# Weights as the moving side: 128-token blocks stationary, 512 weight columns streamed, results with tokens on partitions

## The chip, the cores and the metric

The kernel runs on one core of a Trainium2 chip. The metric is device time in microseconds (us), the median of several executions. One execution was also recorded by the hardware profiler. Its engines are called PE (matrix products), DVE (elementwise, vector), ACT (elementwise with function tables), POOL (here only start values and DMAs that add) and SP (which only issues DMAs). Each engine works through its own instructions in order; an instruction that waits for a semaphore holds up all that follow it on that engine.

## The reference

One layer of a gated encoder trunk, for 512 tokens of width 2048, all in float32:

```
hn    = rmsnorm(x, norm_g)
proj  = hn @ w_in          # 12 heads x (q, k, v, g), 4 forget logits, 3 x 2048 merge gates
gates = sigmoid(proj[merge] + b_gate)
y[n]  = attention_n(q, k, v) * silu(g)       # n = A (forgetting), B (relative bias), C (stick-breaking)
out   = x + (sum_n gates[n] * (y[n] @ w_up[n])) @ w_out
```

A and B normalise every head's q and k over its 128 channels. Each head has 128 channels and there are 4 heads in each of the three branches. The products with `w_in` (12,288 columns and 4 logits), `w_up` (3 times 512 to 2048) and `w_out` (2048 to 2048) are nearly all of the work.

## The kernel before, in words

**Precision.** Every operand of a large product is split into a high and a low part of a shorter float type (`split`, L242: ACT copies the high part, L245; DVE subtracts it, L249). A product is then three: high x high, high x low, low x high.

**Which side moves.** On PE one operand is loaded into the array (stationary, 128 x 128) and the other streams through it. Here a 128 x 128 block of the weight is stationary, `wh` or `wl`, and the activations stream: results have 128 weight columns on partitions and tokens along the row, so q, k, the gate and the merge gates come out channel by channel.

**Strassen tasks.** `PairTask` (L602) takes two column blocks of 128 (q and k of a head, v and g of a head, two neighbouring merge gates, two output blocks) and forms them for the 512 tokens in seven products instead of eight: tokens in two halves of 256, the inner dimension in two halves of 8 x 128, the two column blocks as the third pair. The token sides of the products are the tiles x1, x2, t23, t4 (for the input) and m1, m2, m23, m4 (for the output), made once by DVE and ACT (`combos`, L505; `merged_a`, L1382, and `merged_b`, L1390). The weight sides are sums of 128-column blocks: two of the five loads of a task are followed by a POOL DMA that adds a second block, and DVE makes two more sums (L640, L646).

One product is one **unit**: 8 wide matmuls (L264, `wh` stationary, 512 columns streamed: 256 of the high and 256 of the low part of the token side) and 8 narrow ones (`wl` stationary, 256 columns of the high part). A unit's weights are one raw tile of 128 x 1024, split one or two units ahead of PE (`LA` = 2). There are 52 pair tasks, so 364 units. The products are put together on DVE and ACT (`after_of`, L692: copies, adds, and folds of two halves of 256).

**The stages.** (1) `first_quad`: q, k, v, g of head C0 straight from the unscaled x, four column blocks at a time, no Strassen; `norm_x` meanwhile finds each token's 1/rms, PE spreads it over all partitions (L479), and DVE multiplies x by it (`split_n`, L500) and splits x again. (2) Four merge gate blocks, no Strassen. (3) 44 pair tasks with the attention of 12 heads slipped in between. In A and B `normed` (L885) squares q and k, sums over channels with a matrix of ones on PE (L898, L899), and takes 16 times a chain of seven ACT and five DVE operations of 128 x 512. v is transposed on PE (L1058). (4) `up_units`: y times `w_up`, gated by the sigmoid of the merge gates, added over the branches: 16 blocks. (5) 8 output pair tasks; the first one in the order 1, 5, 2, 3, 6, 7, 4 (`late`), because its sixth token side m23 needs the last block of stage 4.

**What sets the order.** Nothing is scheduled by the compiler. At build time a planner (`Flow`) simulates PE, ACT and DVE with a fixed cost per operation (`mm_us`, `act_us`, `dve_us`) and a model of the DMA queue (`landing`, `add_up`), always takes the task that could start first, and the instructions are written in that order. Tile pools are counted (`Slots`): t2 are rows of 128 x 512, x the split token sides, raw the loaded weights (6 buffers), wh and wl their parts (3 buffers each), acc and att four PSUM banks each.

Of the kernel before, what the change touches and what calls it, by code (L numbers as in the profile page):

```python
# [8 lines left out]
F32 = mybir.dt.float32  # L9
# [6 lines left out]
P = 128  # L16
# [9 lines left out]
UK = 8  # L26
NQ = 4
# [135 lines left out]
def hybrid_kernel(  # L163
# [5 lines left out]
    w_first: bass.AP,  # L169
    w_col: bass.AP,  # L170
    rel: bass.AP,
# [25 lines left out]
    accs = [Slots(2), Slots(1), Slots(1)]  # L197
# [7 lines left out]
    def acc(i=0):  # L205

        return pa.tile([P, S], F32, tag=f"acc{i}", name=nm("acc"), bufs=1 if i else 2)
# [16 lines left out]
    class Parts:  # L224
# [10 lines left out]
        def both(self, i):  # L235

            return self.t[:, i, :, :], self.t[:, i, 0, :], self.ev[i]
# [57 lines left out]
    bg = small_in[:, KT + 5:KT + 5 + NB * DT]  # L295
    wf = small_in[:, KT + 5 + NB * DT:].rearrange("p (k h) -> p k h", h=NH)
# [9 lines left out]
    ones_r = cp.tile([P, P], F32R, name="ones_r")  # L306
    nc.vector.tensor_copy(ones_r, onef)
# [20 lines left out]
    t2s.free.pop()  # L328
# [8 lines left out]
    cur = [0]  # L337

    def at(u, g):
        side.setdefault(u, []).append(g)  # L340

    class Unit:


        def __init__(self, mms, after=None, shape=(UK, P), srcs=()):
# [3 lines left out]
        def source_there(self):  # L349
            return self.there  # L350

        def source(self):
            return self.raw
# [3 lines left out]

    def raw_tile(shape=(UK, P)):
        return wp.tile([P] + list(shape), F32, tag="raw", name=nm("raw"), bufs=NR)

    def load_unit(u):
        if isinstance(u, Pair):
            if u is u.task.units[0]:
                yield from u.task.load()
            return
        for s in u.srcs:
            yield raws, 1
            t = raw_tile(u.shape)
            to = t
            if len(s.shape) > len(t.shape):  # L370
                to = t.rearrange("p (c k) m -> p c k m", c=s.shape[1])
            u.raw = t
            u.there.t = fetch(to, s, flow.ready, 4 * u.shape[0] * P * P // 1024).t

    def prep(u):
        n = u.shape[0] * P
        u.hi = wp.tile([P] + u.shape, F32R, tag="wh", name=nm("wh"), bufs=LA + 1)
        u.lo = wp.tile([P] + u.shape, F32R, tag="wl", name=nm("wl"), bufs=LA + 1)
        yield u.source_there()
        yield from split(u.hi, u.lo, u.source(), n, u.ready, hi_ev=u.ready_hi)  # L380
        u.split_done()
# [7 lines left out]
    norm_ev = [Event() for _ in range(KT)]  # L389
    used_q = [Event() for _ in range(KT)]  # L390
    scaled, f_used = [Event() for _ in range(KT)], [Event() for _ in range(KT)]
    used_g = [Event() for _ in range(UK)]
    x1 = [Parts("x1", [norm_ev[k], Event()]) for k in range(UK)]
    x2 = [Parts("x2", [norm_ev[k + UK]] * 2) for k in range(UK)]
# [12 lines left out]
    xnat = [xp.tile([P, 2, S], F32, tag="x", name=nm("xn")) for _ in range(UK)]  # L407
    n_in = [Event() for _ in range(NQ * QB)]
# [28 lines left out]
    def rsqrt(y, ps, n, tmp, size, done=None):  # L437

        t, w, v = tmp
        yield ACT, act_us(size)  # L440
        nc.scalar.activation(t, ps, AF.Ln, bias=epsc, scale=1.0 / n)
        yield ACT, act_us(size)
        nc.scalar.activation(v, ps, AF.Identity, bias=nhepsc, scale=-0.5 / n)
        if done is not None:
            done()
# [9 lines left out]
    rstd, rstd_ev = [], Event()  # L455
    n_split = [0]

    def norm_x():
# [7 lines left out]
        small_n = cp.tile([P, 5, QB], F32, name="small_n")  # L466
        y, m, tmp = small_n[:, 0, :], small_n[:, 1, :], [small_n[:, i, :] for i in range(2, 5)]
        yield DVE, 0.2
        nc.vector.tensor_reduce(m, ssq, axis=AX.X, op=ALU.add)
        yield from rsqrt(y, m, D, tmp, 4)  # L470
        yield t2s, 1
        dg = t2("dg")
        for b in range(QB):
            yield ACT, 0.3
            nc.scalar.activation(dg[:, blk(b)], identf, AF.Copy, scale=y[:, b:b + 1])
        yield atts, 1
        ps = att()
        yield PE, 0.9
        nc.tensor.matmul(ps, onef, dg, start=True, stop=True)  # L479
        give(t2s, 2)  # L480
        yield t2s, 1
        yield ACT, act_us(S)
        rstd.append(t2("rstd"))
        nc.scalar.activation(rstd[0], ps, AF.Copy)
        give(atts)
        set_(rstd_ev)

    def rstd_used():
        n_split[0] += 1
        if n_split[0] == KT + 5:  # L490
            give(t2s)

    def split_n(kt):

        due = (52.0 + 1.0 * kt + (8 if kt >= UK else 0),)
        yield raw_ev[kt]
        yield rstd_ev
        yield f_used[kt]
        yield (DVE, dve_us(S), *due)
        nc.vector.tensor_mul(xraw[kt], xraw[kt], rstd[0])  # L500
        yield used_q[kt]
        yield from split(xs[kt].hi, xs[kt].lo, two(xraw[kt]), S, norm_ev[kt], due)
        rstd_used()

    def combos(k):  # L505

        due = (96.0 + k,)
        late = (106.0 + k,)
        yield norm_ev[k]
        yield norm_ev[k + UK]  # L510
# [10 lines left out]
        yield used_g[k]  # L521
        h, lo, ev = x1[k].half(1)
        yield from split(h, lo, a[:, LH], HS, ev, due)
# [6 lines left out]
        give(t2s)  # L530
        if k % 2 == 0:
            t4[k // 2] = Parts("t4")
# [4 lines left out]
        give(t2s)  # L537
# [3 lines left out]
    def strassen_ops(x1, x2, t23, t4):  # L541

        def part(ts, i):
            return lambda k: ts[k] and ts[k].both(i)

        return {1: part(x1, 0), 2: part(x2, 0), 3: part(x2, 1), 5: part(x1, 1), 6: part(t23, 0), 7: part(t23, 1),
                4: lambda k: t4[k // 2] and t4[k // 2].both(k % 2)}


    def halves(c):  # L550
        return [w_col[c, 0], w_col[c, 1]]

    def col_task(srcs, evac, bank=0, used=None):

        st = {}

        def mms(i):
            def go(u):
                if i == 0:
                    yield accs[bank], 1  # L560
                    st["ps"] = acc(bank)
                ps = two(st["ps"])
                for j in range(UK):
                    kt = i * UK + j
                    yield norm_ev[kt]
                    yield PE, mm_us(S, 2)
                    mm(ps, u.hi[:, j, :], xs[kt].hi, kt == 0)
                    mm(ps, u.hi[:, j, :], xs[kt].lo)
                yield u.ready
                for j in range(UK):  # L570
                    kt = i * UK + j
                    yield PE, mm_us(S)
                    mm(ps, u.lo[:, j, :], xs[kt].hi, stop=kt == KT - 1)
                    if used is not None and i == 0:
                        set_(used[j])
            return go

        def after():
            yield from evac(st["ps"])
            give(accs[bank])  # L580
        return [Unit(mms(i), after if i == 1 else None, srcs=[srcs[i]]) for i in range(2)]

    class Pair(Unit):


        def __init__(self, task, i):
            super().__init__(task.mms_of(i), task.after_of(i))
            self.task, self.p = task, task.order[i]

        def source_there(self):  # L590
            if self is self.task.units[0]:
                spawn(self.task.sums(), 3.0)
            return self.task.there[self.p]

        def source(self):
            return self.task.w[self.p]

        def split_done(self):
            if self.p in (3, 4, 7):
                give(raws)  # L600

    class PairTask:  # L602
# [9 lines left out]
        def __init__(self, src1, src2, ops, c1_done=None, c2r_done=None, c2_done=None, late=False, rest=None, turns=False):  # L612
            self.src, self.ops, self.late, self.rest, self.turns = (*src1, *src2), ops, late, rest, turns
            self.done = {"c1": c1_done, "c2r": c2r_done, "c2": c2_done}
            self.order = (1, 5, 2, 3, 6, 7, 4) if late else (1, 2, 6, 5, 7, 3, 4)
            self.w, self.there, self.ps = {}, {p: Event() for p in range(1, 8)}, {}
            self.ev = {p: Event() for p in range(1, 8)}
            self.units = [Pair(self, i) for i in range(7)]

        def unit(self, p):  # L620
            return self.units[self.order.index(p)]

        def load(self):
            a11, a12, a21, a22 = self.src
# [957 lines left out]
```

## Time and profile before

| | |
|---|---|
| time, median of 3 runs | 1336.81 us (1336.81 to 1336.93) |
| time of the profiled execution | 1337.21 us |
| its span, first to last instruction | 1335.5 us |
| granted clock of PE, mean | 0.997 |
| DVE busy | 1112.6 us |
| ACT busy | 791.0 us |
| DMA | 263.06 MB, 197 GB/s over the span |

A row of a profile group reads: line, engine, operation, out<-in, shape, xcount | busy us, mean ns of one. Busy time counts overlapping instructions once, while the mean is the whole duration of one; consecutive matmuls overlap, so what one costs in a stream is the distance between starts (its pace). A timeline row reads: start us, duration us, engine, line, operation, out<-in, shape, xcount, and in brackets the idle time ahead of it with the engine that ended it; such a row can merge several instructions.

### The profile page before, as it was taken

How to read it: one execution, taken by the hardware profiler on the slowest of the kernel's cores; microseconds unless marked ns; L12 is line 12 of the kernel's file. 1: busy time of each engine (PE TensorE's matmuls, PEld its weight loads, DVE VectorE, ACT ScalarE, POOL GpSimd, SP SyncE). 2: the span in 40 equal slices, each digit the busy share in tenths (PEclk: the TensorE clock that was granted, in tenths of full speed). 3: DMA queues.
4: the chain of work that ended last, by engine and by line, in shares of the span. 5: the costliest groups of instructions: out<-in, count | busy, mean ns of one | idle time of the engine just before them, and what ended most of it. 6: DMA issues, size and time to landing. Idle time of an engine off the chain costs nothing.

```text
span 1335.5 us, 19770 instructions
## 1 busy us (share of the span) xinstructions
PE 1321.0 (99%) x7364; PEld 1148.0 (86%) x7364; DVE 1112.6 (83%) x1626; ACT 791.0 (59%) x1215; POOL 91.7 (7%) x115
## 2 busy tenths in 40 slices
PE   9999999999999999999999999999999999989998
PEld 7788888888888888888888888888888788878887
DVE  5999998888787887878888888878798877897786
ACT  7656666646566566665666556665577655444443
POOL 0000101000010000100000000000000000001000
PEclk9999999999999999999999999999999999989999
DMA  9556767777767777677767778777778655758883
GB/s 359 178 133 185 175 182 184 192 202 196 197 181 201 187 212 185 185 200 176 224 189 181 195 180 222 180 189 197 190 196 266 224 189 189 197 143 248 233 251 88
DMA packets 89824, 263.06 MB, mean 197 GB/s; under 512 B 10480, under 2 KB 12656, under 8 KB 89728
## 3 DMA queue, kind: packets, MB, share of 16 engines
q1 hardware_dynamic: 71152, 203.00, 45.5%
q0 software_dynamic: 14976, 54.53, 24.6%
q10 hardware_dynamic: 3600, 4.26, 0.9%
q8 instruction: 58, 0.95, 0.3%
q14 instruction: 38, 0.31, 0.1%
HBM read 242.06 MB, written 19.70 MB: 196 GB/s over the span
## 4 chain that ended last, share of the span: by engine, by line
PE 98%; DVE 1%; POOL 0%; issue 0%; ACT 0%; DVEq 0%; ACTq 0%; POOLq 0%
PE acc L264 84%; PE att L264 8%; PE att L995 1%; PE att L1098 1%; PE att L1099 1%; PE att L260 1%; PE att L261 1%; PE att L259 1%; PE att L1097 1%; DVE wl L249 0%; PE att L1058 0%; PE att L403 0%; PE att L1185 0%; PE att L899 0%; PE att L898 0%; DVE m L249 0%
## 5 line engine op out<-in xcount | busy, mean ns | idle before, releaser
L249 DVE TENSOR_TENSOR wl<-raw,wh 128x1024 fp32r<-128x1024 f32 (+2 forms) x413 | 494.5, 1198 | 142.3 <-ACT wh L245 134.3
L245 ACT ACTIVATE wh<-raw 128x1024 fp32r<-128x1024 f32 (+2 forms) x413 | 427.8, 1037 | 163.8 <-PE acc L264 84.1
L264 PE MATMUL acc<-x,wh 128*128 128x512 f32 x1600 | 413.5, 393 | 0.0
L264 PEld LDWEIGHTS acc<-x,wh 128*128 128x128 f32 x1600 | 292.8, 188 | 58.9 <-ACT x L433 0.9
L264 PE MATMUL acc<-t,wh 128*128 128x512 f32 x1056 | 268.6, 393 | 0.0
L264 PEld LDWEIGHTS acc<-x,wl 128*128 128x128 f32 x1504 | 210.3, 190 | 18.5 <-issue 0.5
L264 PE MATMUL acc<-x,wl 128*128 128x256 f32 (+1 forms) x1504 | 223.5, 289 | 0.0
L264 PEld LDWEIGHTS acc<-t,wh 128*128 128x128 f32 x1056 | 189.2, 189 | 32.8
L264 PE MATMUL acc<-t,wl 128*128 128x256 f32 x1056 | 152.7, 284 | 0.0
L264 PEld LDWEIGHTS acc<-t,wl 128*128 128x128 f32 x1056 | 139.6, 191 | 2.2
L280 POOL DMA_DIRECT2D raw<-in_w_col x88 | 76.3, 867 | 922.9 <-DMA raw<-in_w_col 549.9
L264 PE MATMUL acc<-m,wh 128*128 128x512 f32 x448 | 114.0, 396 | 6.3 <-DVE m L249 5.9
L264 PEld LDWEIGHTS acc<-m,wh 128*128 128x128 f32 x448 | 81.7, 191 | 21.7 <-DVE m L249 6.3
L765 ACT ACTIVATE c<-acc 128x256 f32<-128x256 f32 x50 | 19.2, 384 | 95.8 <-PE acc L264 90.8
L743 ACT ACTIVATE u<-acc 128x512 f32<-128x512 f32 x50 | 29.8, 596 | 64.4 <-PE acc L264 64.4
L264 PE MATMUL att<-y,wh 128*128 128x512 f32 x256 | 66.5, 390 | 1.3 <-DVE y L249 1.3
L264 PEld LDWEIGHTS acc<-m,wl 128*128 128x128 f32 x448 | 61.9, 193 | 5.1 <-DVE wl L249 0.8
L640 DVE TENSOR_TENSOR raw<-raw,raw 128x1024 f32<-128x1024 f32 x52 | 63.4, 1220 | 0.4
L264 PE MATMUL acc<-m,wl 128*128 128x256 f32 x448 | 63.4, 285 | 0.4 <-DVE wl L249 0.4
L646 DVE TENSOR_TENSOR raw<-raw,raw 128x1024 f32<-128x1024 f32 x52 | 63.4, 1220 | 0.4
L726 ACT ACTIVATE v<-acc 128x512 f32<-128x512 f32 x52 | 31.1, 599 | 49.2 <-PE acc L264 45.9
L264 PEld LDWEIGHTS att<-y,wh 128*128 128x128 f32 x256 | 47.9, 188 | 12.2 <-DVE y L249 2.5
(183 smaller groups left out, 1359.3 us busy)
## 6 DMA issues: line engine op xcount, KB each, us to landing
raw<-in_w_col SPq DMA_DIRECT2D x228, 512.0 KB, 4.5
raw<-in_w_col POOLq DMA_DIRECT2D x88, 512.0 KB, 6.2
raw<-in_w_out SPq DMA_DIRECT2D x40, 512.0 KB, 4.4
gl<-c SPq DMA_DIRECT2D x48, 256.0 KB, 3.0
raw<-in_w_up SPq DMA_DIRECT2D x32, 384.0 KB, 3.3
sg<-gl SPq DMA_DIRECT2D x48, 256.0 KB, 4.8
raw<-in_w_out POOLq DMA_DIRECT2D x16, 512.0 KB, 6.9
x<-in_xT SPq DMA_DIRECT2D x16, 256.0 KB, 6.0
```

Of the source, the lines that this page charges most:

```text
L245: nc.scalar.activation(hi, src, AF.Copy)
L249: nc.vector.tensor_sub(lo, src, f(hi))
L259: nc.tensor.matmul(ps, lh, rh, start=start, stop=False, skip_group_check=more)
L260: nc.tensor.matmul(ps, lh, rl, start=False, stop=False, skip_group_check=more)
L261: nc.tensor.matmul(ps, ll, rh, start=False, stop=stop, skip_group_check=more)
L264: nc.tensor.matmul(ps, w, x, start=start, stop=stop, skip_group_check=more)
L280: nc.gpsimd.dma_start(to, src, accum_op=ALU.add)
L640: nc.vector.tensor_add(w[1], w[1], w[5])
L646: nc.vector.tensor_add(w[2], w[2], w[1])
L726: nc.scalar.activation(self.v, ps, AF.Copy)
L743: nc.scalar.activation(self.u, ps, AF.Copy)
L765: nc.scalar.activation(c, ps[:, RH], AF.Copy, scale=-1.0)
```

## The change

The two sides of all large products change places. A block of 128 tokens of the split activations is stationary, and 512 weight columns stream. Results have 128 tokens on partitions and 512 columns along the row.

What follows from it:

- **Columns in groups of 512.** A head's q, k, v, g (4 x 128) are one group; 512 merge gates are one group. Head C0 and the first gate group are plain (`quad`). Every other head is paired with a gate group in one Strassen task: 11 tasks for the input, 2 for the output, 13 in all. Each product is cut into four chunks of 2 x 128 inner rows; a chunk is one unit: two inner rows x two token blocks x three matmuls, 12 matmuls of 512 columns. 13 x 7 x 4 = 364 units.
- **Order of a task.** All four chunks of product 5, then 1, 6, 7, 4, 2, 3. Five products load their chunks, two of them with an adding DMA: four such loads in a row for product 5 and four for product 7. The buffers of product 5 are held to product 3, as its sums are made in place (raw: 8 buffers).
- **1/rms at the end.** Tokens lie on partitions, so 1/rms is a number for each partition: ACT scales a head's result by it (`got`), DVE scales a gate's result and adds `b_gate` in one operation (`spill`). `split_n`, L479 and the second split of x are gone. The forget logits are scaled after a small transfer through DRAM.
- **Norms of q and k** are sums along the row: ACT squares 128 x 128 with an accumulator (8 for each head of A and B), and all eight columns share one small chain (`norms`). The matrix of ones is gone.
- **Transposes.** q, k and the gate of each head are now transposed on PE, four blocks each (`turned`); v is not. The gated sum of stage 4 is transposed, 16 times four blocks (`turned_m`). Stage 4 runs by column groups 0, 2, 1, 3.
- **The first output task** runs products 5, 1, 6 for its first two chunks, then for the last two, then the rest.
- **Pools:** wl 2 buffers instead of 3, raw 8 instead of 6, t2 20 instead of 21.

```diff
+    def products(u, ps, kts, tbs, block, first=False, last=False, bank=None, done=None, outer=False):
+        for group in [[tb] for tb in tbs] if outer else [tbs]:
...
+            for j, kt in enumerate(kts):
+                for tb in group:
+                    yield lambda: block(kt, tb) is not None
+                    h, lo, ev = block(kt, tb)
+                    yield ev
+                    yield PE, mm_us(S, 2)
+                    mm(ps[tb], h, u.hi[:, j, :], first and j == 0)
+                    mm(ps[tb], lo, u.hi[:, j, :])
+            yield u.ready
+            for j, kt in enumerate(kts):
+                for tb in group:
+                    yield PE, mm_us(S)
+                    mm(ps[tb], block(kt, tb)[0], u.lo[:, j, :], stop=last and j == len(kts) - 1)
+            if last:
+                for tb in group:
+                    spawn(done(tb), 1.0, flow.fin)
...
+    PLAIN = [(p, c) for p in (5, 1, 6, 7, 4, 2, 3) for c in range(CH)]
...
+        def got(self, tb, c, src):
+            yield rstd_ev
             yield ACT, act_us(S)
+            nc.scalar.activation(c, src, AF.Copy, scale=rstd[:, tb:tb + 1])
...
+        def norms(self):
+            t = sp.tile([P, 5, 2 * QB], F32, tag="norms", name=nm("norms"), bufs=2)
+            y, ss, tmp = t[:, 0, :], t[:, 1, :], [t[:, i, :] for i in range(2, 5)]
+            for tb in (2, 3, 0, 1):
+                yield self.event("c", tb)
+                for r in (K, Q):
+                    i = r * QB + tb
+                    yield ACT, 0.4
+                    nc.scalar.activation(junk, self.c[tb][:, blk(r)], AF.Square, accum_out=ss[:, i:i + 1])
+            yield from rsqrt(y, ss, HD, tmp, 2 * QB)
+            for r in (K, Q):
+                for tb in range(QB):
+                    i = r * QB + tb
+                    yield ACT, 0.25
+                    c = self.c[tb][:, blk(r)]
+                    nc.scalar.activation(c, c, AF.Copy, scale=y[:, i:i + 1])
+                set_(self.event("n", r))
+        def turned(self, r):
+            yield PE, 0.11 * QB
+            ps = att()
+            for tb in range(QB):
+                nc.tensor.transpose(ps[:, blk(tb)], self.c[tb][:, blk(r)], identf)
...
+        order, other = PLAIN, ()
+        if i == 0:
+            order = [(p, c) for cs in ((0, 1), (2, 3)) for p in (5, 1, 6) for c in cs]
+            order += PLAIN[3 * CH:]
+            other = (6,)
+        return Strassen(src, mops, done, order, other, rest).units
...
-NT = 21
+NT = 20
-NR = 6
+NR = 8
```

**Three places in the order of the instructions.** In the rows, the number behind a name tells buffers apart, x2 marks a row that comes twice, and the brackets name the engines waited for.

PE in the middle of a task, before: the end of one unit's wide matmuls and the start of its narrow ones (weights `wh`, `wl` stationary).

```order
L264 MATMUL acc_11787<-m_2125_11704,wh_11725 128x512
L264 MATMUL acc_11787<-m_1933_10723,wl_11726 128x256 [waits DVE_49]
L264 MATMUL acc_11787<-m_1960_10864,wl_11726 128x256
L264 MATMUL acc_11787<-m_1988_11006,wl_11726 128x256
L264 MATMUL acc_11787<-m_2015_11147,wl_11726 128x256
```

PE in the middle of a task now: one whole unit, two token blocks (the two acc banks), two inner rows (x_12, x_13).

```order
L265 MATMUL acc_3666<-wh_3644,x_12_119 128x512 [waits Activation_49]
L265 MATMUL acc_3666<-wh_3644,x_12_119 128x512
L265 MATMUL acc_3667<-wh_3644,x_12_119 128x512 x2
L265 MATMUL acc_3666<-wh_3644,x_13_120 128x512 x2
L265 MATMUL acc_3667<-wh_3644,x_13_120 128x512 x2
L265 MATMUL acc_3666<-wl_3668,x_12_119 128x512 [waits DVE_49]
L265 MATMUL acc_3667<-wl_3668,x_12_119 128x512
L265 MATMUL acc_3666<-wl_3668,x_13_120 128x512
L265 MATMUL acc_3667<-wl_3668,x_13_120 128x512
```

No 256-column matmul is left: 8 + 8 matmuls of a unit have become 12 of 512 columns.

ACT now, in the first head of B, between the squares of q and k and the scaled k (w and v are the head's token blocks; `wh` rows are splits for later units, `vh` the high part of v):

```order
L786 ACTIVATE junk,norms_3664<-w_3578 128x128 [waits Activation_49]
L456 ACTIVATE norms_3664<-norms_3664,epsc 128x8 [waits Activation_49]
L458 ACTIVATE norms_3664<-norms_3664,nhepsc 128x8
L460 ACTIVATE norms_3664<-norms_3664 128x8 [waits Activation_49]
L462 ACTIVATE norms_3664<-norms_3664 128x8 [waits Activation_49]
L366 ACTIVATE wh_3749<-raw_2983 128x1024 [waits DVE_49,PE_49]
L835 ACTIVATE vh_3747<-w_3570 128x128
L793 ACTIVATE w_3570<-w_3570,norms_3664 128x128 [waits DVE_49]
L793 ACTIVATE w_3578<-w_3578,norms_3664 128x128
L793 ACTIVATE v_3273<-v_3273,norms_3664 128x128
L793 ACTIVATE v_3285<-v_3285,norms_3664 128x128
```

and PE at the transposes of that k, two matmuls into the first unit of product 3:

```order
L265 MATMUL acc_3782<-wh_3716,x_10_117 128x512 [waits Activation_49]
L265 MATMUL acc_3782<-wh_3716,x_10_117 128x512
L801 MATMUL att_3794<-identf,w_3570 128x128 [waits PE_49,Activation_49]
L801 MATMUL att_3794<-identf,w_3578 128x128 [waits Activation_49]
L801 MATMUL att_3794<-identf,v_3273 128x128 [waits Activation_49]
L801 MATMUL att_3794<-identf,v_3285 128x128 [waits Activation_49]
L265 MATMUL acc_3783<-wh_3716,x_10_117 128x512 x2
```

The chain ends in four ACT operations for which PE waits in the middle of a unit; before, PE's place behind the squares was the product with the matrix of ones.

PE in the first output task, before: the wide matmuls of product 6, the fifth unit behind stage 4 (m_2117 to m_2152 are m23 of the eight inner rows; the last one needs the last block of stage 4):

```order
L264 MATMUL acc_11818<-m_2117_11688,wh_11754 128x512 [waits PE_49,Activation_49]
L264 MATMUL acc_11818<-m_2118_11689,wh_11754 128x512
L264 MATMUL acc_11818<-m_2119_11690,wh_11754 128x512
L264 MATMUL acc_11818<-m_2120_11691,wh_11754 128x512
L264 MATMUL acc_11818<-m_2121_11692,wh_11754 128x512 [waits DVE_49]
L264 MATMUL acc_11818<-m_2122_11693,wh_11754 128x512 [waits DVE_49]
L264 MATMUL acc_11818<-m_2123_11694,wh_11754 128x512 [waits DVE_49]
L264 MATMUL acc_11818<-m_2152_11851,wh_11754 128x512 [waits DVE_49]
```

and now: the last two chunks of product 6 (m_1986, m_1992, m_2000, m_2006 are m23 of the last four inner rows, made from the last column group), the eleventh and twelfth unit behind stage 4:

```order
L265 MATMUL att_10398<-wh_10503,m_1986_10334 128x512 [waits Activation_49]
L265 MATMUL att_10398<-wh_10503,m_1986_10334 128x512
L265 MATMUL att_10399<-wh_10503,m_1986_10334 128x512 x2
L265 MATMUL att_10398<-wh_10503,m_1992_10366 128x512 x2
L265 MATMUL att_10399<-wh_10503,m_1992_10366 128x512 x2
L265 MATMUL att_10398<-wl_10525,m_1986_10334 128x512 [waits DVE_49]
L265 MATMUL att_10399<-wl_10525,m_1986_10334 128x512
L265 MATMUL att_10398<-wl_10525,m_1992_10366 128x512
L265 MATMUL att_10399<-wl_10525,m_1992_10366 128x512
L265 MATMUL att_10398<-wh_10524,m_2000_10401 128x512 [waits Activation_49]
L265 MATMUL att_10398<-wh_10524,m_2000_10401 128x512
L265 MATMUL att_10398<-wh_10524,m_2006_10429 128x512 x2
```

Six units more stand between the end of stage 4 and the first matmul that needs its last group.

More of the change, by code (lines that the diff above doesn't have):

```diff
@@ L26 @@
 UK = 8
+CH = 4
 NQ = 4
@@ L355, in split_done, with raw_tile @@
         def split_done(self):
             give(raws)
-    def raw_tile(shape=(UK, P)):
+    def raw_tile(shape=(2, S)):
         return wp.tile([P] + list(shape), F32, tag="raw", name=nm("raw"), bufs=NR)
[L361 to L373, printed above, removed]
@@ L465, in norm_x @@
         give(xps, UK)
-        small_n = cp.tile([P, 5, QB], F32, name="small_n")
-        y, m, tmp = small_n[:, 0, :], small_n[:, 1, :], [small_n[:, i, :] for i in range(2, 5)]
+        small_n = cp.tile([P, 4, QB], F32, name="small_n")
+        m, tmp = small_n[:, 0, :], [small_n[:, i, :] for i in range(1, 4)]
         yield DVE, 0.2
         nc.vector.tensor_reduce(m, ssq, axis=AX.X, op=ALU.add)
[L470 to L485, printed above, removed]
-        set_(rstd_ev)
[L488 to L503, printed above, removed]
-    def combos(k):
[L507 to L510, printed above, removed]
+        yield from rsqrt(rstd, m, D, tmp, QB)
+        set_(rstd_ev)
+        nc.sync.dma_start(rd.rearrange("b p -> p b"), rstd)
+    def combos(k):
+        due = (70.0 + 3 * k,)
+        late = (80.0 + 3 * k,)
+        for kt in (k, k + UK):
+            yield raw_ev[kt]
+            yield f_used[kt]
         a, b = xraw[k], xraw[k + UK]
@@ L537, in combos @@
         give(t2s)
+        yield used_g[k]
+        h, lo, ev = x1[k].half(1)
+        yield from split(h, lo, a[:, LH], HS, ev, late)
+        give(t2s)
     t4_ev = [Event() for _ in range(UK // 2)]
@@ L583, in hybrid_kernel, with go @@
[L583 to L596, printed above, removed]
+            def go(k, tb):
+                t = ts[k]
+                return t and (*t.block(2 * i + tb), t.ev[i])
@@ new lines, in split_done, with sum_up @@
+            elif self.p in (1, 2):
+                spawn(self.sum_up(), 4.0)
+        def sum_up(self):
+            task, c = self.task, self.c
+            own, after = (5, 6) if self.p == 1 else (6, 3)
+            to = task.unit(own, c)
+            yield to.ready
+            yield DVE, dve_us(2 * S)
+            nc.vector.tensor_add(to.raw, to.raw, self.raw)
+            give(raws)
+            set_(task.unit(after, c).there)
+    PLAIN = [(p, c) for p in (5, 1, 6, 7, 4, 2, 3) for c in range(CH)]
@@ L1181, in go @@
+                if early and (kts[-1] + 1) % 4 == 0:
+                    four = range(kts[-1] - 3, kts[-1] + 1)
                     for kt in four:
@@ L1400, in merged_b @@
         q = DVE, dve_us(HS)
-        yield xps, 1
-        ev = Event()
-        m2[k] = Parts("m2", [ev, ev])
-        yield from split(m2[k].hi, m2[k].lo, two(b), S, ev)
         yield q
@@ L1480, in loads @@
+    for i in range(2):
+        units.extend(out_task(i))
     def loads():
```

1026 lines of the change are left out of this document (457 added, 569 removed).

## The prediction

> **What bounds the kernel now.** I read the page first: its span, the busy line and the chain that ended last.
>
> ```profile
> span 1335.5 us, 19770 instructions
> PE 1321.0 (99%) x7364; PEld 1148.0 (86%) x7364; DVE 1112.6 (83%) x1626; ACT 791.0 (59%) x1215; POOL 91.7 (7%) x115
> PE 98%; DVE 1%; POOL 0%; issue 0%; ACT 0%; DVEq 0%; ACTq 0%; POOLq 0%
> ```
>
> PE works for 99% of the span and the chain runs over PE for 98% of it. The next view, PE's waits, says what the other per cent is:
>
> ```profile
> PE acc L264 <- DVE m L249: 5.9, 1, 5.9
> PE att L403 <- DVE identb L312: 2.1, 1, 2.1
> PE att L264 <- DVE y L249: 1.3, 2, 1.0
> ```
>
> In all 9.3 us, most of it one wait in the first output task. The third view asks whether other engines have room in the long stage of pair tasks (columns: us, then busy of PE, PEld, DVE, ACT, POOL, then granted clock, DMA share, GB/s):
>
> ```profile
> 500.00:600.00 100.00, 100.00 (x583) 88.45 (x582) 80.43 (x119) 63.33 (x98) 8.65 (x10) 1.00 0.72 190
> ```
>
> PE has no gap in these 100 us, at full clock; DVE has 20 us free, ACT 37, the DMA engines 28%. So the time is what PE is given to stream, plus the places where it waits. An edit on another engine counts only if it makes PE wait.
>
> **The change part by part.** *Units.* Both kernels have 364 of them, and both stream 6144 columns in one: 8 x 512 + 8 x 256 before, 12 x 512 now. What differs is the cost of narrow matmuls. The timeline of PE (start, duration) in the output stage:
>
> ```profile
> 1201.12 2.00 PE L264 MATMUL acc<-m,wh 128*128 128x512 f32 x8
> 1202.96 1.12 PE L264 MATMUL acc<-m,wl 128*128 128x256 f32 x8
> 1203.91 2.00 PE L264 MATMUL acc<-m,wh 128*128 128x512 f32 x8
> ...
> 1223.47 2.00 PE L264 MATMUL acc<-m,wh 128*128 128x512 f32 x8
> ```
>
> From 1201.12 to 1223.47 eight units start: 22.35 / 8 = 2.79 us each. A stream of nothing but 512-column matmuls stands in the chain of waits, stage 4, where a unit of 36 shows as two pieces; every second piece of 24:
>
> ```profile
> 1045.36 5.44 PE att L264 x24
> ...
> 1110.64 5.44 PE att L264 x24
> ```
>
> 65.28 us for 8 units of 36 are 226.7 ns per matmul. Twelve of them are 2.72 us. The new unit lies between 2.72 and the old 2.79; I take 2.73, near the row that has its shape, with 0.01 for the change of stationary side and bank between units. 364 x (2.73 - 2.79) = **-21.8 us**; the bounds are -25.5 and 0.
>
> *Removed from PE.* The matrix of ones, V's transposes and the spread of 1/rms:
>
> ```profile
> 383.90 0.40 PE L898 MATMUL att<-sqh,ones_r 128*128 128x512 f32 x1
> 384.36 0.39 PE L264 MATMUL acc<-t,wh 128*128 128x512 f32 x1
> 1013.49 0.60 PE L1058 MATMUL att<-identf,c 128*128 128x128 f32 x4
> 1013.92 0.38 PE L995 MATMUL att<-identf,p 128*128 128x128 f32 x2
> L479 PE MATMUL att<-dg,tmpc 128*128 128x512 f32 x2 | 1.0, 592 | 0.0
> ```
>
> From the first ones product to the next unit's matmul are 0.46 us (L899 lies between): 16 times is **-7.4**. Four transposes take 0.43 us to the next start: 12 times is **-5.2**. L479 is **-1.0**.
>
> *Added to PE.* q, k and g of 12 heads are 36 groups of four transposes, the gated sum 16 groups. The same pace applies, since it is the same operation in the same kind of stream: 36 x 0.43 = **+15.5**, 16 x 0.43 = **+6.9**. The rows above bound it: a transpose has a duration of its own, 272 ns in the groups:
>
> ```profile
> L1058 PE MATMUL att<-identf,c 128*128 128x128 f32 x48 | 7.2, 272 | 0.0
> ```
>
> If starts stood that far apart instead of 0.43 / 4 = 0.108 us, 208 transposes would cost 34 us more. The starts in the timeline decide for 0.108. The Trainium skill, "TensorE: Matmul & The Clock Gate", Part 4 (PE-mode transpose), gives about 275 ns for a 128 x 128 transpose within a kernel; as a duration the trace agrees (272 ns), as a pace it does not (108 ns).
>
> *The stall in the output task.*
>
> ```profile
> 1183.66 0.80 PE L264 MATMUL acc<-m,wh 128*128 128x512 f32 x1 [5.87 <-DVE m L249]
> 1184.26 1.91 PE L264 MATMUL acc<-m,wl 128*128 128x256 f32 x8
> 1185.96 3.20 PE L264 MATMUL acc<-m,wh 128*128 128x512 f32 x8
> 1189.00 1.11 PE L264 MATMUL acc<-m,wl 128*128 128x256 f32 x8
> ```
>
> PE waits 5.87 us for the last m23, the fifth unit behind stage 4. Then it runs slowly: 1183.66 to 1189.00 are 5.34 us for one wide, eight narrow and eight wide matmuls, which at the pace of 1201.12 take 0.23 + 0.95 + 1.84 = 3.02. So the stall costs 5.87 + 2.3 = 8.2. Now six more units (16.4 us) stand ahead of that matmul, and the wait goes: **-8.2**. What is late next are the first sums m of the last group, which every early unit needs too, behind transposes, a copy and a split on DVE: I take **+1**, between 0 and the 5.87 of the old place. The wait for y (1.3) goes, since stage 4's order leaves its first group alone: **-1.3**.
>
> *New waits.* At the border of stages 3 and 4 the sigmoids of the gates (ACT) now begin only after the last head's output; the nearest rows are the waits of 2.1 and 1.3 above. I take **+2**, from 0 to 4. In A and B, PE's transposes of k and q stand behind the small chain; product 2's four units lie between (rival A): **+2**, from 0 to 8 by the long durations.
>
> *Hidden.* Folds and splits of squares leave DVE, the scaling of 48 spilled gate blocks comes, at the price of an operation of 128 x 512 that reads PSUM:
>
> ```profile
> L711 DVE TENSOR_TENSOR c<-u 128x256 f32<-128x256 f32 x100 | 42.5, 425 | 3.4
> L249 DVE TENSOR_TENSOR sql<-sq,sqh 128x512 fp32r<-128x512 f32 x16 | 11.0, 689 | 1.9 <-ACT sqh L245 1.9
> L735 DVE TENSOR_TENSOR u<-u,acc 128x512 f32<-128x512 f32 x50 | 34.3, 687 | 14.5 <-PE acc L264 14.4
> ```
>
> 48 x 0.687 = 33 against 42.5 + 11.0: DVE gets freer, and its 20% in the window cover it; without the cover the 33 us would be on the path. At the end of the program a result of 512 columns is evicted instead of 256 (0.38 us before), at most 0.4 more; I take 0.
>
> *Sum.* -21.8 - 7.4 - 5.2 - 1.0 + 15.5 + 6.9 - 8.2 + 1 - 1.3 + 2 + 2 = **-17.5**. The profiled execution took 1337.21 us (1.7 us outside its span), 0.4 above the median of the runs: 1319.7 against it, **1319** against the median.
>
> **The rivals.** *A, slower: k comes late in every head of A and B.* PE reaches k's transposes after four units of product 2, one group of transposes for g and two matmuls: 4 x 2.73 + 0.43 + 0.45 = 11.8 us after product 4's last matmul. Meanwhile ACT scales two results, squares eight times, splits three weight tiles, copies g and a part of v, runs the small chain and scales k four times. Rows of ACT for these kinds:
>
> ```profile
> 27.55 0.62 ACT L464 ACTIVATE xn<-xn 128x512 f32<-128x512 f32 x1
> 28.16 0.62 ACT L464 ACTIVATE xn<-xn 128x512 f32<-128x512 f32 x1
> ...
> 30.61 0.28 ACT L441 ACTIVATE small_n<-small_n,epsc 128x4 f32<-128x4 f32 x1
> ...
> 34.29 1.27 ACT L475 ACTIVATE dg<-identf,small_n 128x128 f32<-128x128 f32 x4
> 35.46 0.71 ACT L433 ACTIVATE x<-x,small_in 128x512 f32<-128x512 f32 x1
> ...
> 38.63 1.05 ACT L245 ACTIVATE wh<-raw 128x1024 fp32r<-128x1024 f32 x1
> 39.58 0.62 ACT L245 ACTIVATE x<-x 128x512 fp32r<-128x512 f32 x1
> ...
> L978 ACT ACTIVATE p<-p,mx 128x128 f32<-128x128 f32 x8 | 3.1, 387 | 0.0
> L978 ACT ACTIVATION_READ_ACCUMULATOR p<-p,mx 128x1 f32 x32 | 6.1, 190 | 0.0
> ```
>
> A square with its sum starts every 0.61 us for a duration of 0.62, so one of 128 columns paces at 0.38; a split at 0.95; a scaled copy of 128 at 1.17 / 4 = 0.29; a scaled 512 at 0.61; the chain takes 1.2. By pace: 2 x 0.61 + 8 x 0.38 + 3 x 0.95 + 6 x 0.29 + 1.2 = 10.1 us, in time. By full durations, the accumulator's 0.19 apart: 1.4 + 4.6 + 3.2 + 2.3 + 1.2 = 12.7, so 0.9 late. With two splits more pushed into the chain by late loads (2.1) it is 3.1 late, 8 heads x 3.1 = 25, **1344**. The point: over 2.6 us per head the gain is gone.
>
> *B: adding loads in runs of four.* The queues' rows:
>
> ```profile
> q1 hardware_dynamic: 71152, 203.00, 45.5%
> q0 software_dynamic: 14976, 54.53, 24.6%
> raw<-in_w_col POOLq DMA_DIRECT2D x88, 512.0 KB, 6.2
> ```
>
> 104 adding transfers take 24.6% of 1335.5: 3.16 us of all engines each; the plain ones, 387 pieces of 512 KB, 1.57 each. Four chunks of product 5 or 7 need 4 x 4.73 = 18.9 us, 25 with the landing of 6.2. Eight raw buffers let the first go eight units ahead, and the fourth is used three units later: 11 x 2.73 = 30. In time; but with four plain loads of another product in between (6.3) it is 1.4 late, 26 runs x 1.4 = 36: **1355**. Before, adding loads were spread out, at a share of 0.72.
>
> *C: the unit costs what it did.* If only columns count and the rest of 2.79 comes from the unit's borders, -21.8 is gone: **1341**. Against it speak the 36-matmul units, which have such borders too.
>
> *D: transposes pace at their duration*, +34: **1353**. Against it speak the starts.
>
> *E: no new wait, unit 2.72*: -3.6 for the units and -5 for the waits taken: **1310**.
>
> **How the numbers follow.** Forecast 0.67, E 0.14, A 0.06, B 0.05, C 0.05, D 0.03. The low end is 1309, just under E. The high end must take in the unit's upper bound, C with 1341, and so also the eight heads at 0.9 us late each (1325); A, B and D stay outside, 0.14 in all. Some 0.2% (2.7 us) is what a measurement of this kernel can tell from no change. Faster is the forecast, E and the small half-forms of A and C: 0.83. C and A lie near the border of 1337, so 0.05 for the same and 0.12 for slower.
>
> **What would show it.** Units of 12 matmuls 2.72 to 2.74 us apart say that the first term is right; 2.79 says C. Four transposes 0.43 apart in the timeline decide D. No row of PE waiting for a sum m of over 1 us in the first output task, and a granted clock of 1.00 there, show the stall gone. A, if it comes, is a wait of PE for ACT at k's transposes, eight times; B a wait for wh or wl whose own split waits for raw. The forecast is wrong if the steady stage shows waits of PE for any engine that come back in every task, since 13 tasks of 76 us multiply each of them.

## The result, and the profile after

The changed kernel takes 1319.51 us (median of 4, 1319.39 to 1320.24), 17.3 us less than before: a ratio of 0.9873, 95% interval 0.9856 to 0.989. The forecast was 1319. One execution of a later run, with the merge gates loaded earlier, took 1446.14 us at a granted clock of 0.851 and is left out, so that run's time is the median of the other three.

The page of the changed kernel: span, busy engines, chain.

```profile
span 1317.7 us, 17190 instructions
PE 1307.4 (99%) x6034; PEld 1078.6 (82%) x6034; DVE 1023.4 (78%) x1420; ACT 752.4 (57%) x1271; POOL 91.5 (7%) x115
PE 95%; DMA 2%; ACT 1%; DVE 1%; issue 0%; POOL 0%; ACTq 0%; POOLq 0%; DVEq 0%
```

PE has 13.6 us less to do, still 99% of the span. DVE lost 89 us and ACT 39. The chain now touches DMA, ACT and DVE for some per cent: stretches where a load or a split is only just in time. PE's waits, all of them:

```profile
PE att L417 <- DVE identb L310: 1.9, 1, 1.9
PE acc L265 <- ACT wh L366: 1.4, 1, 1.4
PE acc L265 <- DVE sg L1248: 1.3, 1, 1.3
PE att L265 <- DVE wl L371: 1.1, 1, 1.1
PE att L801 <- ACT w L793: 0.4, 1, 0.4
```

The 5.9 us for m are gone, and nothing above 1.9 us is left. The output stage in PE's timeline, at a place like that of before:

```profile
1250.99 1.98 PE L265 MATMUL acc<-wh,m 128*128 128x512 f32 x8
1252.81 1.07 PE L265 MATMUL acc<-wl,m 128*128 128x512 f32 x4
1253.71 1.98 PE L265 MATMUL acc<-wh,m 128*128 128x512 f32 x8
```

And a stretch of units in its chain of waits (start, length, count):

```profile
1191.56 29.93 PE acc L265 x132
```

A unit is now 1253.71 - 1250.99 = 2.72 us, and 132 matmuls in 29.93 us are 226.7 ns each, the pace of stage 4 before.

The transposes, and what ACT does ahead of k's, in a head of B (ACT's rows first, then PE's):

```profile
573.00 1.06 ACT L366 ACTIVATE wh<-raw 128x1024 fp32r<-128x1024 f32 x1 [2.72 <-DMA raw<-in_w_col]
573.97 1.32 ACT L764 ACTIVATE w<-w,rstd 128x512 f32<-128x512 f32 x2
...
575.39 0.19 ACT L786 ACTIVATION_READ_ACCUMULATOR junk<-v 128x1 f32 x1
575.83 0.19 ACT L786 ACTIVATION_READ_ACCUMULATOR junk<-v 128x1 f32 x1
...
582.50 0.68 ACT L793 ACTIVATE w<-w,norms 128x128 f32<-128x128 f32 x2
583.08 0.68 ACT L793 ACTIVATE v<-v,norms 128x128 f32<-128x128 f32 x2
...
572.65 1.98 PE L265 MATMUL acc<-wh,x 128*128 128x512 f32 x8
...
584.00 0.62 PE L265 MATMUL acc<-wh,x 128*128 128x512 f32 x2
584.45 0.38 PE L801 MATMUL att<-identf,w 128*128 128x128 f32 x2
584.67 0.38 PE L801 MATMUL att<-identf,v 128*128 128x128 f32 x2
584.81 1.64 PE L265 MATMUL acc<-wh,x 128*128 128x512 f32 x6
```

The four scaled blocks of k are done at 583.76, and PE asks for the first at 584.45: 0.7 us to spare. Read in the same way, six of the eight heads of A and B have 0.7 to 0.8 us, one has 0.4, and in the last one k is late: that is the wait of 0.4 at L801. Four transposes take 584.81 - 584.45 = 0.36 us to the start of the next matmul, and the six matmuls behind them 1.64 us, where eight in a stream take 1.98 and so six 1.98 - 2 x 0.227 = 1.53: 0.47 us in all for a group of four. In the starts of the whole trace every group that stands alone costs 0.45 to 0.48, and the 16 transposes in a row in stage 4 cost 1.77 each time; all 52 groups come to 23.8 us, the wait in the last head left out.

### The profile page after: what moved, and what is told of

Its sections match the earlier page's. It is cut to its first block, busy times and chain, and to the rows that moved or that the text cites. A ratio compares the mean times of both kernels' runs of the same rounds, so it can differ in the third digit from the quotient of the medians.

```text
span 1317.7 us, 17190 instructions
## 1 busy us (share of the span) xinstructions
PE 1307.4 (99%) x6034; PEld 1078.6 (82%) x6034; DVE 1023.4 (78%) x1420; ACT 752.4 (57%) x1271; POOL 91.5 (7%) x115
## 4 chain that ended last, share of the span: by engine, by line
PE 95%; DMA 2%; ACT 1%; DVE 1%; issue 0%; POOL 0%; ACTq 0%; POOLq 0%; DVEq 0%
PE acc L265 87%; DMA raw<-in_w_out 2%; PE att L801 1%; PE att L926 1%; PE att L260 1%; PE att L261 1%; PE att L262 1%; DMA raw<-in_w_col 1%; PE att L1016 1%; PE att L1015 1%; PE att L1282 1%; ACT wh L366 1%; PE att L265 1%; PE att L1014 0%; DMA sg<-gl 0%; DVE wl L371 0%
## 5 line engine op out<-in xcount | busy, mean ns | idle before, releaser
L371 DVE TENSOR_TENSOR wl<-raw,wh 128x1024 fp32r<-128x1024 f32 (+1 forms) x405 | 493.4, 1220 | 209.5 <-PE acc L265 122.7
L366 ACT ACTIVATE wh<-raw 128x1024 fp32r<-128x1024 f32 (+1 forms) x405 | 426.7, 1055 | 369.5 <-PE acc L265 283.2
L265 PE MATMUL acc<-wh,x 128*128 128x512 f32 x1664 | 429.5, 392 | 0.0
L265 PEld LDWEIGHTS acc<-wh,x 128*128 128x128 f32 x1664 | 308.8, 188 | 65.7 <-ACT xn L476 1.7
L265 PE MATMUL acc<-wh,t 128*128 128x512 f32 x1056 | 272.7, 391 | 0.0
L265 PE MATMUL acc<-wl,x 128*128 128x512 f32 x832 | 230.1, 390 | 0.0
L265 PEld LDWEIGHTS acc<-wh,t 128*128 128x128 f32 x1056 | 196.7, 188 | 40.3
L265 PEld LDWEIGHTS acc<-wl,x 128*128 128x128 f32 x832 | 155.8, 188 | 33.0 <-DVE wl L371 0.4
L265 PE MATMUL acc<-wl,t 128*128 128x512 f32 x528 | 149.3, 390 | 0.0
L265 PE MATMUL acc<-wh,m 128*128 128x512 f32 x416 | 105.2, 390 | 1.5 <-ACT wh L366 1.4
```

The source lines that it names most:

```text
L265: nc.tensor.matmul(ps, w, x, start=start, stop=stop, skip_group_check=more)
L366: nc.scalar.activation(u.hi, u.raw, AF.Copy)
L371: nc.vector.tensor_sub(u.lo, u.raw, f(u.hi))
```

## The experiments

Each kernel is the changed kernel with one edit. The times are medians, and "more" or "less" is against 1319.51. The kernel before, taken again beside these runs, had medians of 1336.92, 1337.17 and 1337.36, so a difference of one or two us is not clear of noise.

**The low pass in narrow matmuls.**

```diff
-                    mm(ps[tb], block(kt, tb)[0], u.lo[:, j, :], stop=last and j == len(kts) - 1)
+                    for s in (LH, RH):      # Strassen units only
+                        mm(ps[tb][:, s], block(kt, tb)[0], u.lo[:, j, s], stop=end and s.stop == S)
```

> The high x low pass of every Strassen unit (4 matmuls of 512 columns) is cut into 8 of 256 columns; the same columns stream. If narrow matmuls cost more per column (0.119 us for 256 against 0.2267 for 512 in the trace of before), a unit grows by 8 x 0.119 - 4 x 0.2267 = 0.045 us and the time by 364 x 0.045 = 16.5 us: 1336 us, with PE free of new waits. If only columns count and the gain of a unit came from its borders, the time stays within 3 us of 1319.5.

Measured: 1342.2, 22.7 us more (ratio to before 1.0039, 1.0024 to 1.0054). PE's timeline, same stage as above:

```profile
1256.29 2.00 PE L265 MATMUL acc<-wh,m 128*128 128x512 f32 x8
1258.13 1.12 PE L265 MATMUL acc<-wl,m 128*128 128x256 f32 x8
1259.08 2.00 PE L265 MATMUL acc<-wh,m 128*128 128x512 f32 x8
```

The unit is 1259.08 - 1256.29 = 2.79 us again, exactly what it was in the kernel before, although the tokens are still the stationary side. So neither the borders of units nor the change of sides made the gain: the width did, or the number of matmuls that goes with it. This run has 7490 weight loads (PEld), the changed kernel 6034, and no run tells the two apart. The expectation was 6 us low because it counted the narrow matmuls alone. They take 0.95 us for eight, where the four wide ones of the changed kernel take 0.90 (1252.81 to 1253.71); but the eight wide ones beside them also take longer, 1.84 instead of 1.82. The Trainium skill, "TensorE: Matmul & The Clock Gate", Part 2 (Back-to-back issue gap), gives 262 cycles for 256 columns and 518 for 512 as the gap of a single matmul, 2.5 ns more for two halves than for a whole; by that the estimate for this kernel would be 364 x 4 x 2.5 ns = 3.6 us, and the 22.7 measured do not agree. That section of the Trainium skill itself calls this the gap of one matmul alone, and says that in a stream the weight loads set the spacing too.

**Every added transpose twice.**

```diff
-                nc.tensor.transpose(ps[:, blk(tb)], self.c[tb][:, blk(r)], identf)
+                for _ in range(2):
+                    nc.tensor.transpose(ps[:, blk(tb)], self.c[tb][:, blk(r)], identf)
...
-            nc.tensor.transpose(ps[:, blk(tb)], merged[g, tb][:, blk(i)], identf)
+            for _ in range(2):
+                nc.tensor.transpose(ps[:, blk(tb)], merged[g, tb][:, blk(i)], identf)
```

> Every one of the 208 added transposes is issued twice into the same place. If they cost their pace (0.43 us for four), 208 more are +22 us: 1342. If each costs its duration of 0.272 us, +57: 1376. If they hide beside other work of PE, the time stays at 1319.5.

Measured: 1339.71, 20.2 us more, 97 ns for each of 208. PE's timeline at the transposes of g in the same head:

```profile
586.51 0.60 PE L802 MATMUL att<-identf,w 128*128 128x128 f32 x4
586.94 0.60 PE L802 MATMUL att<-identf,v 128*128 128x128 f32 x4
587.30 1.17 PE L265 MATMUL acc<-wh,x 128*128 128x512 f32 x4
```

Eight transposes take 0.79 us to the next matmul, where four took 0.36: 0.108 us for each one added, the pace, or 22.5 us for 208. The total is lower, in part because the wait for k has gone from this run. They cost their pace, and rival D is out.

**Every square twice.**

```diff
-                    nc.scalar.activation(junk, self.c[tb][:, blk(r)], AF.Square, accum_out=ss[:, i:i + 1])
+                    for _ in range(2):
+                        nc.scalar.activation(junk, self.c[tb][:, blk(r)], AF.Square, accum_out=ss[:, i:i + 1])
```

> Every square of k and q with its sum is issued twice on ACT, which the planner does not know, so the order of PE stays. In the trace the last scaled k ends 0.7 us ahead of k's transposes (583.76 against 584.45) and a square starts every 0.43 us. If rival A's mechanism is real and only just missed, eight more squares make k 8 x 0.43 - 0.7 = 2.7 us late in each of 8 heads: +22 us, 1341, and PE waits for ACT at L801. If ACT's idle time takes the extra work up, under +4.

Measured: 1339.8 (1337.61 to 1341.56), 20.3 us more. PE's waits in it:

```profile
PE att L802 <- ACT w L794: 10.4, 8, 2.2
PE acc L265 <- ACT wh L366: 2.9, 4, 1.5
```

The same head's k in PE's timeline:

```profile
588.98 0.61 PE L265 MATMUL acc<-wh,x 128*128 128x512 f32 x2
590.76 0.62 PE L802 MATMUL att<-identf,w 128*128 128x128 f32 x2 [1.16 <-ACT w L794]
591.35 0.62 PE L802 MATMUL att<-identf,v 128*128 128x128 f32 x2
591.72 1.64 PE L265 MATMUL acc<-wh,x 128*128 128x512 f32 x6
```

Eight waits, one for each head of A and B, at the transposes that rival A named. The rows call only 10.4 us a wait; a part of the rest is the transposes themselves, which now come one by one as ACT delivers (590.76 to 591.72 is 0.96 us, where 0.36 stood). By starts, 588.98 to 591.72 is 2.74 us where the changed kernel has 0.81 (584.00 to 584.81): 1.93 us a head, an estimate of 15.4 in eight heads. The rest of the 20.3 is elsewhere: waits for wh, 2.9 us instead of 1.4, and in the profile two stretches at half the clock (0.50 in 1018.00:1021.00 and in 1267.20:1270.50), which the changed kernel does not have. Rival A's mechanism is real; the expected 2.7 us a head was too much, and the total came near it by these other parts. The changed kernel misses the mechanism by 0.7 us in most heads.

**The last column group needed at the old place.**

```diff
-            order = [(p, c) for cs in ((0, 1), (2, 3)) for p in (5, 1, 6) for c in cs]
+            order = [(p, c) for cs in ((2, 3), (0, 1)) for p in (5, 1, 6) for c in cs]
```

> The first output task does its last two chunks first: the last chunks of product 6, which need the last column group, move from the eleventh and twelfth place behind stage 4 back to the fifth and sixth, where the stall stood before. If the place removed the stall, a wait of PE for m comes back there; in the changed kernel's trace the last two m23 are ready at 1172.9 and 1174.9, and the sixth unit would use them from 1173.0 and 1173.9: 1 to 3 us of wait, with the lower clock behind it 1321 to 1325 in all. If m23 is now made earlier for another reason and the place is worth nothing, 1319.5 within 1.

Measured: 1324.36 (1320.78 to 1326.47), 4.9 us more. The profiled execution is the fastest of the four, 1320.78, with a granted clock of 1.000; the other three, from 1324.0 on, had 0.996 to 0.997. PE's timeline in the sixth unit behind stage 4:

```profile
1171.71 1.19 PE L265 MATMUL att<-wh,m 128*128 128x512 f32 x4 [1.00 <-DVE m L250]
1174.39 0.96 PE L265 MATMUL att<-wh,m 128*128 128x512 f32 x3 [1.48 <-DVE m L250]
```

The wait for m is back, in the unit that was expected, with 1.00 + 1.48 us, less than half of the 5.87 of before. In this execution that costs 1.3 us in all, as the wait of 1.1 for wl has gone. The median's 4.9 goes with the lower clock of the other three, and no trace shows where they lost it. So the place is worth 1.3 us where the clock holds and 4.5 to 7.0 in the executions where it does not. The rest of the 5.87 may have gone because m is ready earlier behind the end of stage 4; no run took that part by itself.

**Seven raw buffers.**

```diff
-NR = 8
+NR = 7
```

> Seven raw buffers in place of eight: every load may start one unit (2.72 us) later. Rival B said four adding loads need 25 us and have 30. If that margin is as large as it was worked out, 27 are still enough: 1319.5 within 2. If the margin is the 2 us or so that ACT's waits for raw (up to 3.4 us, against a lead of two units) leave, PE waits at the start of products 5 or 7 in most tasks: 26 x 0.5 to 26 x 1 = +13 to +26.

Measured: 1412.8, 93.3 us more, far outside both. PE's waits:

```profile
PE acc L265 <- ACT wh L366: 49.3, 26, 4.7
PE acc L265 <- DVE wl L371: 9.7, 10, 1.4
```

One task in the timeline (PE, ACT, then the queue of SP):

```profile
510.24 1.20 PE L265 MATMUL acc<-wh,t 128*128 128x512 f32 x4 [1.91 <-ACT wh L366]
511.50 1.22 PE L265 MATMUL acc<-wl,t 128*128 128x512 f32 x2
512.52 1.91 PE L265 MATMUL acc<-wh,t 128*128 128x512 f32 x4
514.22 0.87 PE L265 MATMUL acc<-wl,t 128*128 128x512 f32 x2
...
598.02 1.20 PE L265 MATMUL acc<-wh,t 128*128 128x512 f32 x4 [1.92 <-ACT wh L366]
599.28 0.74 PE L265 MATMUL acc<-wl,t 128*128 128x512 f32 x2
...
509.13 2.95 ACT L366 ACTIVATE wh<-raw 128x1024 fp32r<-128x1024 f32 x3 [8.30 <-DMA raw<-in_w_col]
...
483.30 14.93 SPq L277 DMA_DIRECT2D raw<-in_w_col  x2
```

ACT waits 8.3 us for a load of product 7; SP's queue shows two loads that take 14.9 us to issue, first to last, the second one held. The unit at 510.24 is the fourth and last chunk of product 7 (four units of product 4 follow before the next x rows), and the long wait stands at this chunk in every task. That fits three buffers for four adding loads.

After the wait PE runs slowly for a while: the four matmuls at 512.52 take 1.70 us to the next row instead of 0.91, and the first of two windows shows the clock at half. The second window holds the wait of 1.92 us one task later:

```profile
511.40:514.70 3.30, 3.24 (x9) 2.53 (x9) 2.56 (x4) 0.68 (x1) 0.00 (x0) 0.50 0.67 195
595.00:605.00 10.00, 8.02 (x34) 5.97 (x33) 6.97 (x9) 5.04 (x6) 0.00 (x0) 1.00 0.63 205
```

There the clock stays at 1.00. (The first four matmuls behind the wait take 1.26 us both times, so that is not the clock.) A wait of 1.9 us can thus cost more than itself, but does not always. The two rows of waits are 59.0 us; the granted clock of the profiled execution, 0.985, makes another 20 by an estimate of 0.015 x 1307 us of busy PE. The planner counts the buffers too, so a part of the order of instructions changes with them; this run does not take that apart.

**Seven raw buffers, no adding loads.**

```diff
-NR = 8
+NR = 7
...
-            if more is not None:
+            if more is not None and False:
                 ev = add_up(self.raw, task.src(*more, c), ev.t, 512)
```

> Seven raw buffers again, and the 104 adding DMAs are left out (products 5 and 7 then use one block where the sum of two belongs). With seven buffers the time rose by 93 us, with waits of PE of 2 to 4 us for the first chunk of product 7 in every task. Product 5 holds four buffers from its own loads to product 3, so product 7's four adding loads have three to go through. If the length of these adding loads is what comes late (rival B's mechanism, at three buffers instead of the eight that B counted), the waits go and the time is 1319 to 1325. If three free buffers are too few for any loads, 1380 or more stays.

Measured: 1321.24, 1.7 us more. Without the second half of these loads seven buffers are enough. (With them, the long waits stood at the last chunk of product 7, not at its first.) So the 93 us come with the adding loads: rival B's mechanism, one buffer away. This run takes away their length and their traffic together, and no run spread them out over the task, so that it is the runs of four that matter is argued, not shown.

**Nine raw buffers.**

```diff
-NR = 8
+NR = 9
-NT = 20
+NT = 18
```

> Nine raw buffers, paid for with two t2 rows (18 instead of 20). If eight are just enough, a ninth gains only the wait for wh at 1245 (1.4 us, with the slower clock behind it 2 at most): 1317.5 to 1319.5. If two rows less make the attention late, 1321 or more.

Measured: 1318.24, 1.3 us less: PE waits no more for wh at 1245, but 2.5 us for merge gates instead of 1.3. The step from seven to eight is worth 93 us, that from eight to nine 1.3, which is not clear of noise.

**More work on DVE.**

```diff
+        if src is c:
+            nc.vector.scalar_tensor_tensor(c, c, 0.0, c, op0=ALU.mult, op1=ALU.add)
         nc.vector.scalar_tensor_tensor(c, src, rstd[:, tb:tb + 1], brows[i], op0=ALU.mult, op1=ALU.add)
```

> The 44 gate blocks that are spilled from a Strassen task are first written onto themselves by one more DVE operation of 128x512, unknown to the planner: 44 x 0.69 = 30 us more work on DVE. If DVE has cover as the prediction said, the time stays within 3 us of 1319.5. If DVE's fall by 89 us is part of the gain, about a third of that comes back: over +8 us.

Measured: 1325.55, 6.0 us more, between the two. PE's and ACT's timeline in a head of C:

```profile
193.57 1.20 PE L265 MATMUL acc<-wh,x 128*128 128x512 f32 x4 [1.14 <-ACT wh L366]
...
278.06 1.20 PE L265 MATMUL acc<-wh,x 128*128 128x512 f32 x4 [1.14 <-ACT wh L366]
...
191.34 0.53 ACT L977 ACTIVATE p<-p 128x384 f32<-128x384 f32 x1 [6.42 <-DVE p L974]
...
192.47 1.99 ACT L366 ACTIVATE wh<-raw 128x1024 fp32r<-128x1024 f32 x2
```

The same operation of ACT in the changed kernel:

```profile
189.56 0.53 ACT L977 ACTIVATE p<-p 128x384 f32<-128x384 f32 x1 [4.47 <-DVE p L974]
```

DVE is not full, but its order is fixed: the added operations push back the attention's p, ACT waits 6.4 us for p, where it waited 4.5, with the split of the next weights behind it, and PE waits 1.1 us for that split. The same wait comes in the next heads of C (278 and 362 us). It is the queue on ACT, not DVE's busy share, that lets it through.

**Merge gates loaded earlier**, and the same with nine raw buffers:

```diff
-        yield last_head.event("hl", 2)
+        yield last_head.event("hl", 0)
```

> The merge gates of stage 4 are loaded from the event of the last head's first attention part instead of its third. In the trace PE waits 1.3 us at 1032 for a gate whose load landed late. If that load sets the wait, 1318; if ACT's sigmoids behind the last head set it, 1319.5; if the loads now take t2 rows from the last head, 1320 to 1325.

> Nine raw buffers, 18 t2 rows and the earlier loads of the merge gates. If both waits of PE (1.3 at 1033, 1.4 at 1245) go with nothing in their place, 1316 to 1318; if rows are short at the border of stages 3 and 4, 1320 or more.

Measured: 1318.06 for the first (ratio to before 0.9856, 0.9839 to 0.9872) and 1317.18 for both (1316.98 to 1317.59; 0.985, 0.9834 to 0.9867). The gates' earlier load gives 1.5 us by itself, which is not clear of noise, and the two edits together beat the changed kernel by 2.3 us, about what a measurement can tell. PE's waits with both:

```profile
PE acc L265 <- DVE sg L1248: 2.1, 2, 1.1
PE att L417 <- DVE identb L310: 1.9, 1, 1.9
PE att L265 <- DVE wl L371: 1.1, 1, 1.1
```

The wait for wh has gone. That for the gates has not: 2.1 us in two pieces of at most 1.1, where 1.3 in one stood. With nine buffers alone it was 2.5, so the earlier loads took 0.4 off it, while the time fell by 1.1; whether the two t2 rows that nine buffers cost keep the rest of it was not tried.

## Why the prediction was right, point by point

- **Units, -21.8.** Right in size, and in that narrow matmuls cost more: undone on its own, the width gives back 22.7. Whether that is the width or the weight load of each matmul stays open. Rival C fell with it, since the sides stayed exchanged and the gain went.
- **Transposes, +22.4.** +20.2 when doubled, 23.8 by the starts of the changed kernel's own trace, 0.45 to 0.48 for a group alone instead of 0.43. The choice between 0.43 / 4 and 0.272 us was the right one, and it rested on starts in the timeline against a mean duration in the groups.
- **Ones, V, L479, -13.6.** These rows are gone from the profile; they were not tried apart.
- **The stall, -8.2.** Gone, and the granted clock is 1.00 there (1170.00:1180.00); in the kernel before it was 0.50 from 1182 to 1188, the slow stretch behind the stall. The reason given, six more units ahead of the last m23, holds for the part that came back: 2.5 us of wait and 1.3 of time in the profiled execution, 4.9 by the median. What was named as late next, a sum m, was not: PE waits 1.1 us there for wl, a weight split standing behind the splits of m on DVE.
- **New waits, +2 and +2.** The border of stages 3 and 4 shows 1.3 for a gate, k one wait of 0.4. Taken too high by some 2 us; the wait of 1.4 for wh in the output stage, which no step named, takes that place.
- **Rival A.** Time to spare was 1.7 us by pace; 0.7 was measured in most heads. PE came as worked out: 572.65, behind product 4, to 584.45 are 11.8 us. ACT's work was no longer than added up either: 573.97 to 583.76 are 9.8 us, where 10.1 stood, and the eight squares take 3.0 us of them, 0.38 each, as taken (two with no split between them start 0.44 apart). What the sum left out is the start. ACT scales the first result 1.3 us behind product 4's last matmul: it is at a weight split then (573.00), and DVE has to finish the sum. The working itself has two slips: 0.9 + 2.1 is 3.0 and not 3.1, and a gain of 17.5 is gone at 2.2 us a head, not 2.6. The price was too high by the rows of the doubled squares, 1.9 us a head where 2.7 was expected.
- **Rival B.** Right that it would not come, but by a wrong step: "Eight raw buffers let the first go eight units ahead". Product 5 keeps four of them up to product 3, so only four circulate, and the margin of 5 us that was worked out does not exist: with one buffer less the price is 93 us, not the 36 for the case at all. The landing of 6.2 us was also short: the 88 adding loads of the input tasks land after 8.0 now (median). That eight buffers were enough was luck as far as this step goes, and 0.05 was too low a chance for a case that stood one buffer away.
- **Hidden.** "Its 20% in the window cover it" was too simple. DVE did get freer, and the step did no harm, but 30 us more on DVE cost 6.0: a busy share does not tell which operation ACT waits for with a weight split behind it.
- **The sum.** -17.5 forecast, -17.3 measured. Put together from what was measured, with the price of a doubled transpose, it closes less well: -22.7 + 20.2 - 13.6 - 9.5 for the two old waits + 4.2 for the four new ones is -21.4. With the 23.8 of all 52 groups by their starts as the second term it is -17.8. That the forecast is within 0.2 is closer than its terms are: units and waits came out better, by 0.9 and 0.8 us, the transposes 1.4 worse, and these offset each other.

## What to carry to other kernels

When PE is busy for 99% and the number of streamed columns stays, look at the width of the matmuls and measure their pace by starts in the trace: here the same columns in 512 instead of 256 were worth 22.7 us. Before trusting a margin in buffers, count those that are held as well as those that circulate; take one away to see how far the edge is. Busy shares say that an engine has room, not that the one operation for which the next engine waits has it.

## What was not expected of the hardware

Wide matmuls are slower beside narrow ones: eight of 512 columns start the next group after 1.84 us when eight of 256 stand between them, after 1.82 when four of 512 do. In the single starts of that trace the loss lies in the first five of the eight, 0.229 to 0.235 us apart; the last three stand at 0.227. A transpose behind another costs 0.108 us, with a duration of about 0.272. And the clock can fall by a short wait of PE: behind one of 1.9 us it was granted at half for some 3.3 us, behind another of the same length it was not.
